# Token halves for the last two blocks of x, recounted scheduler costs and new ranks in a hybrid decoder layer

## The chip, the core and the metric

The kernel runs on one core of one Trainium2 chip. The metric is the device time of one execution in microseconds, as the median of three runs. The engines are TensorE (PE, with its weight loads as PEld), VectorE (DVE), ScalarE (ACT), GpSimd (POOL) and SyncE (SP), which issues all loads and stores here.

## The reference

One decoder layer over 1,024 tokens of width 1,024, in float32:

```python
mod = silu(c) @ w_ada + b_ada                    # shift, scale, gate, 1024 each
h = rms_norm(x, norm_w) * (1 + scale) + shift
u_pool, g_pool, q, k, v, g_attn, qi, ki, wi = split(h @ w_in)   # 2888 columns
pool_out = pool_mixer(u_pool, w_pool, pool_scale) * silu(g_pool)  # running means over 2, 4, 8, 16 tokens
q, k = rope(rms_norm(q)), rope(rms_norm(k)); qi, ki = rope(qi), rope(ki)
# per block of 128 queries: index scores, the 256 best keys of each query, softmax over those
score = sum_h relu(qi_h . ki) * wi_h;  sel = top_k(score, 256)
attn_out = softmax(q . k[sel]) @ v[sel] * silu(g_attn)
x = x + gate * (concat(pool_out, attn_out) @ w_out)
```

## The kernel before

The 1,024 channels of x lie in eight blocks of 128 partitions by 1,024 tokens (xt). The work comes in stages.

**Start.** `token_sums` (lines 505 to 564) loads x block by block, squares each block on ScalarE (sq), and adds the squares over all channels. A block in `SUMS` (0, 2, 4) goes to TensorE by itself as eight one-column products (128x1, one per 128 tokens, against a column of ones); the other blocks are first added on VectorE, and their sum goes to TensorE as eight more. The last block alone is loaded, squared and added in two token halves, tokens 512 to 1,023 first. `token_scales` turns the sums into 1/rms, by square root on ScalarE, reciprocal on VectorE and eight transposes on TensorE that spread it over the partitions (rsb). `lead_loads` and `modulations` meanwhile reduce the 16 blocks of w_ada (wa) for shift and scale on VectorE.

**Lead.** For each block j, `first_block` or `h_block` makes xn = x * rsb, then h as a high part (hhi) and a low part (hlo), so that a product can be had as three fast ones (hi*hi, hi*lo, lo*hi). `lead_line` then computes four tiles of the index queries over all eight blocks at once. GpSimd multiplies xn for blocks 1 to 7 and makes the low halves of the weights (wl); VectorE makes hlo. `SCALED` lists blocks whose xn is made on VectorE instead (none). Key and value rows follow.

**Middle.** `gates`, `queries` and `pool_mixer` compute the other projections in a fixed order, mixed with the index scores (kiT). The choice of the 256 best keys is a bisection over the bits of the score, on VectorE (junk) for query blocks 2 to 4 and on ScalarE (ajunk) for 5 to 7. `pool_mixer` ends in a high and a low part per group (mph, mpl).

**Attention and output.** `unit` does one query block: scores (kT,qr), a masked copy with row maxima on VectorE (ex, mx), exponentials on ScalarE, transposes of ex, and products with the values (pw,vrow). `gated` multiplies by the gate and splits the result (mah, mal). `output_line` runs beside it as filler: `project_pooled` first, then `project_attended(0)` for tokens 0 to 511 when query blocks 0 to 3 are done, and `project_attended(1)` at the very end.

**What sets the order.** The whole order is made when the program is built. Every strand of work is a generator that yields operations; `Flow.run` (line 415) takes at each step the strand whose operation can start first by a model of times, shifted by a rank: `EARLY` by name (or by name and number) for VectorE, ScalarE, GpSimd and SP, `LAST` by kind for TensorE, `SAFE` as a slack that a TensorE operation wants behind its data. `Op._cost` (line 150) holds the costs; `Op.data` (line 182) says when operands and outputs are free; `Either` picks between two engines with `FAVOUR` and `BACK`. Nothing of this runs on the chip: there the engines work through their lists in order and wait on semaphores.

All helper-issued instructions carry one line in the profile, L216 (L223 in the changed program), so that groups are told apart by tile names.

Of the kernel before, what the change touches and what calls it, by code (L numbers as in the profile page):

```python
# [17 lines left out]
P = 128  # L18
S = 1024
NT = 8  # L20
# [19 lines left out]
         "pick": -0.6, "mix": -0.33, "rotated": 0.12, "query_loads": 0.01, "exps": -0.11, "score_sums": -1.13,  # L40
         "key_value_out": -1.67, "index_queries": -1.47, "norm": -2.65, "gate_loads": 0.5, "token_scales": -0.26,
         "gate_mods": -0.39, "unit": -0.41, "index_scores": -0.67, "lead_loads": 1.25, "out": -1.53,
         "lead_out": -0.72, "weight_loads": -0.67, "key_value_weights": -0.07, "main_line": 0.66,
# [8 lines left out]
         "key_value_out 7": -1.92, "exps 5": -0.08, "key_value_out 4": -3.2, "query_norms": 0.51, "exps 8": 0.04,  # L52
# [7 lines left out]
         "products": -1.29, "shift 4": -0.32, "norm 5": -1.88, "low 1": -0.9, "turns 6": -2.43, "gated 6": -1.5,  # L60
         "turns 8": -2.26}
# [5 lines left out]
SAFE = {"side": 1.0, "unit": 0, "query_norms": 0, "h_block": 0.59, "rotated": 0.73, "query_loads": 0,  # L67
        "norm": 0.0, "weight_loads": 1.18, "key_value_out": 0.39, "turned": 0.26, "finish": 0.07, "index_keys": 0,
        "main_line": 0, "output_line": 0, "gate_mods": 1.07, "selection": 0, "low": 0, "maxima": 0,
        "attention": 0.05, "lead_out": 0, "score_relus": 0.1, "lead_loads": 0.28, "score_sums": 0.18, "mix": 0.96,  # L70
        "main": 0, "modulations": 0.09, "out": 0.39, "turns": 0, "exps": 0}
# [9 lines left out]
PHOP = -0.09  # L81
STT = 0.075
# [16 lines left out]
MIX = 4  # L99
# [20 lines left out]
class Op:  # L120


    def __init__(self, eng, name, fn, args, kw):
        self.eng, self.name, self.fn, self.args, self.kw = eng, name, fn, args, kw
        aps = [a for a in args if isinstance(a, bass.AP)]
        named = [a for k, a in kw.items() if isinstance(a, bass.AP)]
        self.outs, self.ins = [], []
        for a in aps[:1] + [kw[k] for k in ("accum_out",) if kw.get(k) is not None]:
            self.outs.append(store(a))
            if a.free_size() == 1:  # L130
                self.outs.append((store(a), a.offset))
# [18 lines left out]
    def _cost(self, aps, kw):  # L150
        size = [a.free_size() for a in aps]
        n = max(size)
        eng = self.eng
        if eng == "SP":
            return 0.42
        if eng == "PE":
            rate = 2 if self.name == "transpose" else 4 if aps[1].dtype == F32 else 1
            if self.name != "transpose" and min(aps[0].shape[0], aps[1].shape[0]) == 64:
                self.mode = "rows" if aps[1].shape[0] == 64 else "columns"
                return size[0] * 0.000417 * rate / 2 + 0.007  # L160
            return max(0.109, size[0] * 0.000417 * rate + 0.0135)
        wide = [a for a, k in zip(aps, size) if k == n]
        psum = any(a.space == PSUM for a in wide)
        half = all(mybir.dt.size(a.dtype) == 2 for a in wide)
        if eng == "ACT":
            t = 0.000833 * n + (0.05 if psum else 0.094)
            t += 0.093 * sum(isinstance(kw.get(k), bass.AP) for k in ("scale", "bias", "accum_out"))
            return t
        if eng == "POOL":
            if self.name == "tensor_tensor":  # L170
                return 0.0021 * n + 0.147
            return 0.000833 * n + 0.16
        if self.name in ("tensor_scalar", "tensor_copy"):
            if "accum_out" in kw:
                return 0.00104 * n + 0.13
            if half:
                return 0.00026 * n + 0.069
            if not psum:
                return 0.00052 * n + 0.069
        return 0.00104 * n + 0.069 + (STT if psum and self.name == "scalar_tensor_tensor" else 0.0)  # L180

    def data(self, flow):
# [4 lines left out]
        for a in self.outs:  # L187
# [209 lines left out]
def hybrid_layer(ctx, tc, xT, cT, nwT, badaT, wada, wq, wet, wkv, qnw, knw, wpool,  # L397
# [107 lines left out]
    def token_sums():  # L505
# [32 lines left out]
        halves = [slice(512, 1024), slice(0, 512)]  # L538
# [3 lines left out]
        added = [j for j in range(NT) if j not in SUMS]  # L542
        acc, started = None, set()
        for j in range(NT):
            sq = yield big(s="sq")
            for c in (halves if j == NT - 1 else [slice(0, 1024)]):
                yield A.activation(sq[:, c], xt[j][:, c], AF.Square)
                if j in added and acc is not None:
                    yield V.tensor_tensor(acc[:, c], acc[:, c], sq[:, c], op=OP.add)
                if j in SUMS or j == added[-1]:  # L550
                    t = sq if j in SUMS else acc
                    for h, half in enumerate(halves):
                        if half.start >= c.start and half.stop <= c.stop:
                            for b in range(4):
                                o = half.start + b * P
                                yield mm(tab["sums"][h][:, b:b + 1], t[:, o:o + P], ones,
                                         h not in started, j == NT - 1 and b == 3)
                                started.add(h)
            if j in SUMS or acc is not None:
                flow.drop(sq)  # L560
# [160 lines left out]
    def lead_line():  # L721
# [3 lines left out]
        for j in range(NT):  # L725
# [23 lines left out]
            flow.drop(whi, wlo)  # L749

# [29 lines left out]
    def weight_splits():  # L780
        for n in range(4 + 16 + 24):
# [678 lines left out]
    def main_line():  # L1460
        yield from lead_line()
# [27 lines left out]
    flow.spawn(weight_splits(), "weights")  # L1489
    flow.spawn(main_line(), "main")  # L1490
# [109 lines left out]
```

## Time and profile before

| | |
|---|---|
| median of 3 runs | 525.88 us (525.6 to 526.51) |
| the profiled execution | 525.81 us, its span 524.1 us |
| TensorE busy | 500.9 us, 96% of the span |
| VectorE, ScalarE, GpSimd busy | 421.7, 381.7, 134.9 us |
| mean granted TensorE clock | 0.993 |

A matmul's busy time overlaps that of the next one, so a busy TensorE is not TensorE at its peak; its waits are read from the view that lists what an engine waited for and from the order of time, where starts of neighbours can be compared.

### The profile page before, as it was taken

The page shows a single profiled execution, that of the slowest core. Times are in us where ns is not written, and L with a number is a line of the kernel's source. Part 1 is how long each engine was busy: PE and PEld are TensorE (multiplying, and loading weights), DVE is VectorE, ACT ScalarE, POOL GpSimd, SP SyncE. Part 2 cuts the span into 40 slices and gives each one's busy share as a digit, 9 for nine tenths or more (in the row PEclk, how much of TensorE's full clock was granted, in tenths as well). Part 3 has the DMA queues.
Part 4 walks back from the last instruction along what each step waited for, and adds up shares of the span by engine and source line. Part 5 has one row for each costly group of instructions (what it writes and reads, how often), then busy time and mean ns, then how long its engine had stood idle before and what let it go on. Part 6 is the DMA issues. An engine that isn't in the chain of part 4 may idle for free.

```text
span 524.1 us, 7765 instructions
## 1 busy us (share of the span) xinstructions
PE 500.9 (96%) x2568; PEld 380.8 (73%) x2568; DVE 421.7 (80%) x902; ACT 381.7 (73%) x868; POOL 134.9 (26%) x154
## 2 busy tenths in 40 slices
PE   6789999999999999989999997999998999999997
PEld 5778899767778868868878775886655756646585
DVE  1799895799789799999999998779896788975142
ACT  6488641687777989979953986899999826877520
POOL 1499430001001223345032431422210124200000
PEclk9999999999999999999999997999999999999999
DMA  8996513010214130211110114673521414301054
GB/s 307 403 408 214 203 45 115 22 61 21 83 28 153 41 87 34 81 40 42 41 41 20 40 43 149 200 250 125 181 82 41 141 60 155 107 21 41 1 161 161
DMA packets 28025, 58.31 MB, mean 111 GB/s; under 512 B 3792, under 2 KB 7888, under 8 KB 27984
## 3 DMA queue, kind: packets, MB, share of 16 engines
q1 hardware_dynamic: 27984, 57.81, 32.6%
q8 instruction: 20, 0.33, 0.3%
q14 instruction: 21, 0.17, 0.1%
HBM read 47.32 MB, written 10.49 MB: 110 GB/s over the span
## 4 chain that ended last, share of the span: by engine, by line
PE 61%; DVE 26%; ACT 7%; issue 4%; POOL 1%; DMA 1%; SPq 0%; DVEq 0%; ACTq 0%
PE m L216 61%; DVE junk L216 10%; ACT ex L216 3%; DVE selw L216 2%; DVE nx L216 2%; DVE sw L216 2%; DVE xq L216 1%; DVE ex L216 1%; DVE aq L216 1%; ACT ajunk L216 1%; DVE gp L216 1%; DVE wl L216 1%; DVE qr L216 1%; DVE mpl L216 1%; DVE u L216 1%
## 5 line engine op out<-in xcount | busy, mean ns | idle before, releaser
L216 PE MATMUL m<-hhi,wh 128*128 128x512 f32 (+1 forms) x320 | 120.3, 398 | 4.0 <-ACT hhi L216 4.0
L216 PE MATMUL m<-hhi,wl 128*128 128x512 f32 (+1 forms) x320 | 115.2, 382 | 0.0
L216 PE MATMUL m<-hlo,wh 128*128 128x512 f32 (+1 forms) x320 | 114.0, 380 | 0.0
L216 ACT ACTIVATE ajunk<-key,xq 128x768 bf16<-128x768 uint16 (+2 forms) x93 | 96.4, 1036 | 2.4 <-DVE xq L216 1.5
L216 PEld LDWEIGHTS m<-hhi,wh 128*128 128x128 f32 x320 | 59.0, 190 | 20.6 <-ACT hhi L216 4.9
L216 DVE TENSOR_SCALAR_CACHE_REDUCE junk<-key,xq 128x384 bf16<-128x384 uint16 (+2 forms) x93 | 69.1, 743 | 2.0
L216 PEld LDWEIGHTS m<-hhi,wl 128*128 128x128 f32 x320 | 59.3, 190 | 12.1 <-issue 1.4
L216 PEld LDWEIGHTS m<-hlo,wh 128*128 128x128 f32 x320 | 58.5, 188 | 12.4 <-DVE hlo L216 0.8
L216 POOL TENSOR_TENSOR wl<-ld,wh 128x512 fp32r<-128x512 f32 x38 | 54.0, 1423 | 43.7 <-ACT wh L216 35.5
L216 ACT ACTIVATE ex<-ex,mx,c 128x384 f32<-128x384 f32 (+7 forms) x64 | 54.9, 859 | 6.5 <-DVE mx L216 6.4
L216 ACT ACTIVATE kt<-m 128x512 f32<-128x512 f32 (+1 forms) x80 | 37.5, 526 | 10.6 <-DVE score L216 6.9
L216 DVE SCALAR_TENSOR_TENSOR score<-kt,c,score 128x1024 f32<-128x1024 f32 (+5 forms) x42 | 39.9, 950 | 6.5 <-ACT kt L216 4.4
L216 DVE SCALAR_TENSOR_TENSOR xo<-m,c,xo 128x512 f32<-128x512 f32 x28 | 21.0, 748 | 24.6 <-PE m L216 19.7
L216 PE MATMUL m<-kT,qr 64*128 64x512 f32 (+3 forms) x192 | 37.9, 512 | 1.6 <-DVE mx L216 1.5
L216 PE MATMUL m<-c,ex 128*128 128x128 f32 x288 | 34.4, 274 | 0.6 <-ACT ex L216 0.3
L216 PEld LDWEIGHTS m<-c,ex 128*128 128x128 f32 x288 | 31.5, 141 | 4.1 <-DVE mx L216 1.4
L216 ACT CAST wh<-ld 128x512 fp32r<-128x512 f32 x36 | 22.0, 615 | 16.3 <-PE m L216 10.8
L216 POOL TENSOR_SCALAR wh<-ld 128x512 fp32r<-128x512 f32 x23 | 15.7, 683 | 69.1 <-PE m L216 58.1
L216 PE MATMUL m<-pw,vrow 128*64 128x512 f32 x144 | 32.7, 598 | 0.0
L216 PEld LDWEIGHTS m<-kT,qr 64*128 64x128 f32 x192 | 18.6, 192 | 18.8 <-issue 11.0
L216 DVE CUSTOM_DVE_ANT_0 ex<-m,key 128x512 f32<-128x512 f32 (+1 forms) x48 | 30.9, 662 | 0.5 <-PE m L216 0.3
L216 PE MATMUL m<-mah,wh 128*128 128x512 f32 x64 | 25.8, 404 | 2.5 <-ACT mah L216 1.3
(190 smaller groups left out, 1036.5 us busy)
## 6 DMA issues: line engine op xcount, KB each, us to landing
wa<-wada SPq DMA_DIRECT2D x24, 512.0 KB, 7.5
ld<-wet SPq DMA_DIRECT2D x16, 512.0 KB, 3.3
ld<-wout SPq DMA_DIRECT2D x24, 256.0 KB, 2.8
xo<-xT SPq DMA_DIRECT2D x16, 256.0 KB, 3.4
y_d<-xo SPq DMA_DIRECT2D x16, 256.0 KB, 2.6
xo<-y_d SPq DMA_DIRECT2D x16, 256.0 KB, 3.3
outT<-xo SPq DMA_DIRECT2D x16, 256.0 KB, 2.2
xt<-xT SPq DMA_DIRECT2D x7, 512.0 KB, 6.6
```

The costliest lines, as they stand in the source:

```text
L216: self.fn(*self.args, **self.kw)
```

## The change

Three things are done, and the numbers that steer the scheduler are replaced throughout.

First, blocks 6 and 7 of x are loaded, squared and added in token halves: both second halves (tokens 512 to 1,023) first, then both first halves. `SUMS` becomes (1, 4), so that 24 one-column products stand where 32 stood.

```diff
-        for j in range(NT):
-            t = yield big(s="xt")
-            for c in ([slice(512, 1024), slice(0, 512)] if j == NT - 1 else [slice(0, 1024)]):
-                yield SP.dma_start(t[:, c], xT[j][:, c])
-            xt.append(t)
+        halves = [slice(512, 1024), slice(0, 512)]
+        pieces = [(j, slice(0, 1024)) for j in range(6)] + [(j, c) for c in halves for j in (6, 7)]
+        for j, c in pieces:
+            if len(xt) == j:
+                xt.append((yield big(s="xt")))
+            yield SP.dma_start(xt[j][:, c], xT[j][:, c])
...
+        sq, acc = {}, None
+        for j, c in pieces:
+            if j not in sq:
+                sq[j] = yield big(s="sq")
+            yield A.activation(sq[j][:, c], xt[j][:, c], AF.Square)
+            if j in SUMS:
+                yield from sums(sq[j], c, False)
+            elif acc is None:
+                acc = sq[j]
+                continue
+            else:
+                yield V.tensor_tensor(acc[:, c], acc[:, c], sq[j][:, c], op=OP.add)
+                if j == NT - 1:
+                    yield from sums(acc, c, True)
```

Second, the scheduler's model: a one-column product of float32 counts as 0.427 us, and an operation that writes one column of a table waits for that column's last users, not for the whole table's.

```diff
-        self.outs, self.ins = [], []
+        self.outs, self.ins, self.over = [], [], []
...
+            self.over.append(self.outs[-1] if a.space != PSUM else store(a))
...
-            return max(0.109, size[0] * 0.000417 * rate + 0.0135)
+            return max(0.427 if rate == 4 else 0.109, size[0] * 0.000417 * rate + 0.0135)
...
-        for a in self.outs:
+        for a in self.over:
             if self.eng == "PE":
```

Third, `lead_line` is a strand of its own that spawns `main_line` at its end, and the first four weight splits are a strand `lead_splits`, so that both have ranks of their own. Of the tables, a few lines:

```diff
-SCALED = ()
+SCALED = (7,)
-SUMS = (0,2,4,)
+SUMS = (1, 4,)
...
-LAST = {"main": 0.12, "fill": 0.113, "scores": -0.039, "attend": -0.078, "evac": -0.027, "qi": 0.284,
-        "side": -0.239}
+LAST = {"main": 0.12, "fill": -0.037, "scores": 0.035, "attend": -0.085, "evac": -0.027, "qi": 0.294,
+        "side": -0.55}
...
-QK = 3
-IK = 3
+QK = 2
+IK = 1
...
-PV = 3
+PV = 5
```

The order that comes out differs on every engine. Three places follow, as the built program lists them.

VectorE right behind the token sums (c_93 is 1/rms, wa a block of w_ada, xn and hlo those of block 0). Before:

```order
L216 RECIPROCAL c_93<-c_93 128x4
L216 SCALAR_TENSOR_TENSOR wa_209,c_89<-wa_209,m 128x1024
L216 RECIPROCAL c_93<-c_93 128x4
L216 SCALAR_TENSOR_TENSOR wa_211,c_89<-wa_211,m 128x1024
L216 TENSOR_SCALAR c_89<-c_89,c_78 128x1
L216 SCALAR_TENSOR_TENSOR wa_214,c_89<-wa_214,m 128x1024
L216 SCALAR_TENSOR_TENSOR xn_243<-xt_108,c_90,m 128x512
L216 SCALAR_TENSOR_TENSOR wa_219,c_89<-wa_219,m 128x1024
L216 SCALAR_TENSOR_TENSOR hlo_245<-xn_243,c_89,hhi_244 128x512
L216 SCALAR_TENSOR_TENSOR wa_221,c_89<-wa_221,m 128x1024
```

Now:

```order
L223 RECIPROCAL c_93<-c_93 128x4
L223 SCALAR_TENSOR_TENSOR wa_205,c_89<-wa_205,m 128x1024
L223 TENSOR_SCALAR c_90<-c_89,c_78,c_77 128x1
L223 SCALAR_TENSOR_TENSOR wa_207,c_89<-wa_207,m 128x1024
L223 SCALAR_TENSOR_TENSOR xn_252<-xt_108,c_90,m 128x512
L223 RECIPROCAL c_93<-c_93 128x4
L223 SCALAR_TENSOR_TENSOR hlo_254<-xn_252,c_89,hhi_253 128x512
L223 SCALAR_TENSOR_TENSOR xn_252<-xt_108,c_90,m 128x512
L223 SCALAR_TENSOR_TENSOR wa_210,c_89<-wa_210,m 128x1024
L223 SCALAR_TENSOR_TENSOR hlo_254<-xn_252,c_89,hhi_253 128x512
```

Block 0 (both halves of xn and hlo) now stands behind two or three blocks of w_ada, not behind three to seven.

The low parts of the pooled mixer, at the start of attention (mph_3297 and mph_3332 are group 0, which the output projection reads first). Before, on VectorE:

```order
L216 CAST mph_3297<-gp_2904 128x1024
L216 TENSOR_SCALAR junk_3287,cq_692_3280<-key_85,xq_688_3266 128x640
L216 ISA ex_3299,mx_2669<-m,mask_82 128x128
L216 ISA mx_2669 128x1
L216 ISA ex_3299,mx_2669<-m,mask_82 128x128
L216 ISA mx_2669 128x1
L216 ISA ex_3296,mx_2671<-m,mask_82 128x256
L216 ISA mx_2671 128x1
L216 TENSOR_TENSOR mpl_3301<-gp_2366,mph_3300 128x1024
L216 ISA ex_3299,mx_2669<-m,mask_82 128x128
L216 ISA mx_2669 128x1
L216 TENSOR_TENSOR mpl_3298<-gp_2904,mph_3297 128x1024
```

Now, on GpSimd:

```order
L223 TENSOR_SCALAR wh_3294<-ld_3167 128x512
L223 TENSOR_SCALAR yq_706_3316<-xq_690_3269 128x3
L223 TENSOR_TENSOR wl_3295<-ld_3167,wh_3294 128x512
L223 TENSOR_TENSOR mpl_3336<-gp_2681,mph_3335 128x1024
L223 TENSOR_TENSOR mpl_3333<-gp_2887,mph_3332 128x1024
```

Group 0's low part has moved from VectorE to GpSimd, behind a weight chunk and behind group 3's low part.

TensorE behind the last query block (pw,vrow), where the final output projection begins. Before:

```order
L216 MATMUL m<-pw_4997,vrow_643 64x512 x2
L216 MATMUL m<-pw_5008,vrow_643 64x512 x2
L216 MATMUL m<-mah_4419,wh_4542 128x512
L216 MATMUL m<-mah_4419,wl_4543 128x512
L216 MATMUL m<-mal_4420,wh_4542 128x512
```

Now:

```order
L223 MATMUL m<-pw_4993,vrow_637 64x512 x2
L223 MATMUL m<-mah_3851,wh_4820 128x512
L223 MATMUL m<-mah_3851,wl_4821 128x512
L223 MATMUL m<-mal_3852,wh_4820 128x512
L223 MATMUL m<-mah_3851,wh_4820 128x512
L223 MATMUL m<-mah_3851,wl_4821 128x512
L223 MATMUL m<-mal_3852,wh_4820 128x512
L223 MATMUL m<-mah_4465,wh_4843 128x512
```

Six products of tokens 0 to 511 (mah_3851, ready since query block 3) now stand between the last attention products and the first product that needs the last query block (mah_4465). In the same way eight kT,qr products stand behind query block 3, where mah followed at once; and of the 96 products of `project_attended(0)` fewer stand beside query blocks 4 and 5, more beside 6 and 7.

## Rows read from the trace of the kernel before

**Rows 1.** The page's first line and its part 1: busy time of an engine, share of the span, instructions.

```profile
span 524.1 us, 7765 instructions
...
PE 500.9 (96%) x2568; PEld 380.8 (73%) x2568; DVE 421.7 (80%) x902; ACT 381.7 (73%) x868; POOL 134.9 (26%) x154
```

**Rows 2.** TensorE alone in a stretch of the lead: stretch, its length, busy time (instructions), granted clock as a share of full, share of the DMA engines, GB/s.

```profile
33.00:62.50 29.50, 29.50 (x170) 1.00 0.71 254
```

**Rows 3.** The start in order of time (all engines): start us, length us, engine, line, operation, written tile <- read tiles, shapes, how many were merged, and in brackets the idle time before it and what ended that. sq are squares of a block, c small constants (here also the scale of the tokens), m is PSUM.

```profile
7.15 13.79 PE L216 MATMUL m<-c,sq 128*128 128x1 f32 x64 [0.52 <-ACT sq L216]
...
9.31 1.06 ACT L216 ACTIVATE sq<-xt 128x1024 f32<-128x1024 f32 x1 [0.22 <-DMA xt<-xT]
...
10.59 1.06 ACT L216 ACTIVATE sq<-xt 128x1024 f32<-128x1024 f32 x1 [0.22 <-DMA xt<-xT]
...
12.96 3.96 DVE L216 TENSOR_TENSOR sq<-sq,sq 128x1024 f32<-128x1024 f32 x4 [1.33 <-ACT sq L216]
...
19.27 0.26 ACT L216 ACTIVATE c<-m,c 128x4 f32<-128x4 f32 x1 [4.01 <-PE m L216]
...
20.80 1.95 PE L216 MATMUL m<-c,c 128*128 128x128 f32 x8
...
23.86 0.74 DVE L216 SCALAR_TENSOR_TENSOR xn<-xt,c,m 128x512 f32<-128x512 f32 x1
...
25.41 2.08 PE L216 MATMUL m<-hhi,wh 128*128 128x512 f32 x4 [2.67 <-ACT hhi L216]
...
30.30 0.74 PE L216 MATMUL m<-hhi,wh 128*128 128x256 f32 x4 [1.30 <-ACT hhi L216]
```

**Rows 4.** ScalarE in the same view, the two half squares of the last block.

```profile
14.13 1.13 ACT L216 ACTIVATE sq<-xt 128x512 f32<-128x512 f32 x2
```

**Rows 5.** VectorE alone in two stretches, columns as in rows 2: the lead, and the stretch up to the start of attention.

```profile
21.30:58.70 37.40, 36.71 (x49) 1.00 0.80 296
186.00:319.00 133.00, 129.04 (x291) 1.00 0.16 50
```

**Rows 6.** Groups of instructions of VectorE in the lead: count, busy us, mean ns of one, idle time before them.

```profile
L216 DVE SCALAR_TENSOR_TENSOR wa<-wa,m 128x1024 f32<-128x1024 f32 x15 | 17.9, 1209 | 0.0
L216 DVE TENSOR_TENSOR hlo<-xn,hhi 128x1024 fp32r<-128x1024 f32 x7 | 11.8, 1691 | 0.5 <-ACT xn L216 0.5
```

**Rows 7.** GpSimd's groups in the lead, same columns.

```profile
L216 POOL TENSOR_TENSOR xn<-xt,rsb 128x1024 f32<-128x1024 f32 x7 | 20.2, 2893 | 0.0
L216 POOL TENSOR_TENSOR wl<-ld,wh 128x512 fp32r<-128x512 f32 x7 | 12.5, 1793 | 0.0
```

**Rows 8.** End of the lead, VectorE, then (next group) TensorE, in order of time.

```profile
57.45 1.21 DVE L216 TENSOR_TENSOR hlo<-xn,hhi 128x1024 fp32r<-128x1024 f32 x1
```

**Rows 9.** TensorE at the same place: the first product that reads the low half of the last block.

```profile
58.72 0.50 PE L216 MATMUL m<-hlo,wh 128*128 128x512 f32 x1
```

**Rows 10.** What TensorE waited for over the whole span: us in total, times, longest.

```profile
PE m L216 <- DVE u L216: 1.8, 2, 1.5
PE m L216 <- DVE mx L216: 1.5, 1, 1.5
PE m L216 <- DVE mpl L216: 1.5, 1, 1.5
PE m L216 <- ACT mah L216: 1.3, 1, 1.3
PE m L216 <- DVE mah L216: 1.2, 1, 1.2
PE m L216 <- ACT pw L216: 0.7, 1, 0.7
```

**Rows 11.** TensorE at the start of attention, in order of time. kT,qr are the first attention scores, mph and mpl the output projection's first inputs.

```profile
313.81 1.37 PE L216 MATMUL m<-kT,qr 64*128 64x128 f32 x16
...
317.83 0.40 PE L216 MATMUL m<-mph,wl 128*128 128x512 f32 x1
319.69 0.80 PE L216 MATMUL m<-mpl,wh 128*128 128x512 f32 x1 [1.47 <-DVE mpl L216]
```

**Rows 12.** GpSimd at the same place: a weight chunk's high half, and its low half.

```profile
311.25 0.62 POOL L216 TENSOR_SCALAR wh<-ld 128x512 fp32r<-128x512 f32 x1 [0.93 <-PE m L216]
...
313.77 1.27 POOL L216 TENSOR_TENSOR wl<-ld,wh 128x512 fp32r<-128x512 f32 x1
```

**Rows 13.** VectorE at the same place.

```profile
318.42 2.35 DVE L216 TENSOR_TENSOR mpl<-gp,mph 128x1024 fp32r<-128x1024 f32 x2
```

**Rows 14.** TensorE in three stretches there, columns as in rows 2.

```profile
315.00:320.00 5.00, 2.06 (x11) 0.88 0.83 250
320.00:325.00 5.00, 5.00 (x14) 0.50 0.33 117
325.00:330.00 5.00, 5.00 (x29) 0.94 0.34 105
```

**Rows 15.** TensorE after the attention of query block 3: pw,vrow are its last products, mah the next work.

```profile
398.98 3.65 PE L216 MATMUL m<-pw,vrow 128*64 128x512 f32 x16
403.85 0.50 PE L216 MATMUL m<-mah,wh 128*128 128x512 f32 x1 [1.21 <-DVE mah L216]
```

**Rows 16.** TensorE after the attention of the last query block, same columns.

```profile
492.44 4.46 PE L216 MATMUL m<-pw,vrow 128*64 128x512 f32 x20
498.16 0.50 PE L216 MATMUL m<-mah,wh 128*128 128x512 f32 x1 [1.25 <-ACT mah L216]
```

More of the change, by code (lines that the diff above doesn't have):

```diff
@@ L39 @@
          "mods": -0.2, "select": -0.1, "scores": -0.6, "attend": -1.1, "late": 1.0, "kv": -0.3, "qi": -0.8,
[L40 to L43, printed above, removed]
@@ L44 @@
-         "output_line": -0.14, "turns": -1.46, "finish": -1.64, "index_keys": -1.47, "h_block": 0.28,
-         "attention_keys": -0.36, "turned": -1.72, "h_blocks": -0.3, "gated": -2.15, "modulations": -0.22,
-         "low": -0.4, "gear": -0.3, "attention": 0.31, "maxima": -0.99, "score_relus": -0.66, "gated 7": -1.82,
[5 rows of a table removed]
-         "key_value_out 7": -1.92, "exps 5": -0.08, "key_value_out 4": -3.2, "query_norms": 0.51, "exps 8": 0.04,
[7 rows of a table removed]
-         "products": -1.29, "shift 4": -0.32, "norm 5": -1.88, "low 1": -0.9, "turns 6": -2.43, "gated 6": -1.5,
@@ L61 @@
-         "turns 8": -2.26}
+         "pick": -0.6, "mix": -0.33, "rotated": 1.0, "query_loads": -0.28, "exps": -0.11, "score_sums": -1.13,
+         "key_value_out": -1.67, "index_queries": -1.47, "norm": -1.6, "gate_loads": -1.2, "token_scales": -3.22,
+         "gate_mods": -0.39, "unit": -0.41, "index_scores": -0.91, "lead_loads": 0.74, "out": -1.53,
+         "lead_out": -0.72, "weight_loads": 0.17, "key_value_weights": 0.67, "main_line": 0.66, "output_line": 0.91,
+         "turns": -1.46, "finish": -1.64, "index_keys": -1.47, "h_block": 0.28, "attention_keys": -0.36,
@@ new lines @@
+         "turned": -1.01, "h_blocks": -2.07, "gated": -2.15, "modulations": -0.38, "low": 0.65, "gear": -0.3,
+         "attention": -0.86, "maxima": -0.99, "score_relus": -0.66, "gated 7": -1.82, "gated 3": -1.0,
[5 rows of a table added]
+         "key_value_out 7": -1.92, "exps 5": -0.25, "key_value_out 4": -3.2, "query_norms": 0.16, "exps 8": 0.04,
[7 rows of a table added]
+         "gear 4": 0.68, "products": -1.29, "shift 4": -0.32, "norm 5": -1.86, "low 1": -2.52, "turns 6": -2.43,
+         "gated 6": -1.5, "turns 8": -1.76, "h_block 3": 0.04, "shift": -0.01, "gear 8": -2.5, "lead_line": 1.29,
@@ L63 @@
+         "gear 7": -1.58, "index_queries 3": -3.45, "index_queries 1": -2.08, "lead_splits": -0.23, "shift 5": -0.05,
+         "first_block": -2.64, "shift 2": 0.74, "lead_out 1": -1.22, "shift 8": 1.3, "out 7": -0.3, "unit 3": -1.17,
+         "turns 3": -2.02, "key_value_out 1": -2.25, "exps 4": -0.27, "mix 2": -0.25}
 SELECT = -0.366
-LAST = {"main": 0.12, "fill": 0.113, "scores": -0.039, "attend": -0.078, "evac": -0.027, "qi": 0.284,
-        "side": -0.239}
+LAST = {"main": 0.12, "fill": -0.037, "scores": 0.035, "attend": -0.085, "evac": -0.027, "qi": 0.294,
+        "side": -0.55}
@@ L67 @@
 SAFE = {"side": 1.0, "unit": 0, "query_norms": 0, "h_block": 0.59, "rotated": 0.73, "query_loads": 0,
[L68 to L71, printed above, removed]
@@ L73 @@
-SCALED = ()
-SUMS = (0,2,4,)
-WKM = 5
+        "norm": 0, "weight_loads": 1.18, "key_value_out": 0.39, "turned": 0.26, "finish": 0.07, "index_keys": 0,
+        "main_line": 0, "output_line": 0, "gate_mods": 1.06, "selection": 0, "low": 0.27, "maxima": 0,
+        "attention": 0.44, "lead_out": 0, "score_relus": 0, "lead_loads": 0.28, "score_sums": 0.18, "mix": 0.96,
+        "main": 0, "modulations": 0.09, "out": 0.39, "turns": 0.34, "exps": 0, "lead_line": 0.6, "shift": 0,
+        "token_scales": 0.08, "index_scores": 0.19, "products": 0, "index_queries": 0.34}
@@ L80 @@
+SCALED = (7,)
+SUMS = (1, 4,)
+WKM = 6
 HOP = 0.103
-PHOP = -0.09
-STT = 0.075
+PHOP = -0.148
+STT = 0.078
 HOPS = {"PE": 0.19, "DVE": 0.13, ("ACT", "DVE"): 0.14, ("ACT", "ACT"): 0.035}
@@ L87 @@
 AGE = 0.37
-PW_POOL = 0.303
+PW_POOL = 0.088
 XO_POOL = 0.108
-BACK = 0.5
-SPAN = 0.115
-QK = 3
-IK = 3
+BACK = 0.768
+SPAN = 0.104
+QK = 2
+IK = 1
 FK = 0
 PK = 0
-MIX = 4
+GM = 4
+MIX = 5
 KEEP = 7
 FLY = 2
-PV = 3
-WA_AHEAD = 5
-AHEAD = 2
+PV = 5
+WA_AHEAD = 3
+AHEAD = 5
 XN_AHEAD = 2
-FAVOUR = {"DVE": 0.235, "ACT": -0.057, "POOL": 0.244}
+FAVOUR = {"DVE": 0.245, "ACT": -0.062, "POOL": 0.244}
 TABLES = {AF.Silu: 1, AF.Sqrt: 2, AF.Exp: 3}
@@ L536, in token_sums @@
         tab["scp"] = psum[:, 0:1024]
-        halves = [slice(512, 1024), slice(0, 512)]
         tab["sums"] = []
@@ L541, in token_sums, with sums @@
             tab["sums"].append((yield bank(4)))
[L542 to L560, printed above, removed]
-            else:
-                acc = sq
-            if j == added[-1]:
-                flow.drop(acc)
+        started = set()
+        def sums(t, c, last):
+            for h, half in enumerate(halves):
+                if half.start >= c.start and half.stop <= c.stop:
+                    for b in range(4):
+                        o = half.start + b * P
+                        yield mm(tab["sums"][h][:, b:b + 1], t[:, o:o + P], ones, h not in started, last and b == 3)
+                        started.add(h)
+        sq, acc = {}, None
[8 more added lines that the diff above has]
+                continue
+            else:
+                yield V.tensor_tensor(acc[:, c], acc[:, c], sq[j][:, c], op=OP.add)
+                if j == NT - 1:
+                    yield from sums(acc, c, True)
+            if c.start == 0:
+                flow.drop(sq[j])
+        flow.drop(acc)
     def token_scales():
@@ L749, in lead_line @@
             flow.drop(whi, wlo)
+        flow.spawn(main_line(), "main")
     def lead_out(e, acc):
@@ L778, in weight_loads, with lead_splits, weight_splits @@
             loaded.append((t, 512, 1))
-    def weight_splits():
-        for n in range(4 + 16 + 24):
+    def lead_splits():
+        yield from weight_splits(range(4))
+        flow.spawn(weight_splits(range(4, 4 + 16 + 24)), "weights")
+    def weight_splits(which):
+        for n in which:
             yield lambda: len(loaded) > n
@@ L1460, in main_line @@
     def main_line():
-        yield from lead_line()
         kv["v"] = yield big(s="vrow")
@@ L1488, in hybrid_layer @@
     flow.spawn(weight_loads(), "weights")
-    flow.spawn(weight_splits(), "weights")
-    flow.spawn(main_line(), "main")
+    flow.spawn(lead_splits(), "weights")
+    flow.spawn(lead_line(), "main")
     flow.spawn(gate_mods(), "late")
```

2 lines of the change are left out of this document (1 added, 1 removed), and 24 rows, old and new, of the table EARLY.

## The prediction

> **What bounds the kernel now.** The profiled execution took 525.81 us, 0.07 below the median of 525.88, so a sum made against the one holds for the other. About 0.2%, 1.05 us, is what a measurement of this kernel can tell from no change.
>
> I began with the busy times. TensorE is busy in 96% of the span [rows 1]: no edit here takes products of the main work away, so time can come only from where TensorE stands idle or runs at less than its full clock. Second I read the start in order of time. Blocks of x land 1.28 us apart (squares begin at 9.31 and 10.59), but TensorE's one-column products run without a gap from 7.15 to 20.94; the 64 records are 32 products (the float32 ones leave two records each), so one takes 13.79 / 32 = 0.431 us. The sums are bound by the number of products, not by the loads: the last half squares are done at 15.26 [rows 4], the first square root comes at 19.27, the transposes at 20.80, block 0's xn at 23.86 and TensorE's first main product at 25.41, with a hole before 30.30 [rows 3].
>
> Third, what feeds the lead. TensorE has no gap from 33.0 to 62.5 [rows 2], but VectorE is busy 36.71 of 37.40 us there [rows 5]. Its last low half begins at 57.45 and ends at 58.66 [rows 8]; the product that reads it begins at 58.72 [rows 9]. Most of VectorE's time is in 15 blocks of w_ada at 1.209 and 7 hlo at 1.691 [rows 6], GpSimd's in 7 xn at 2.893 and 7 wl at 1.793 [rows 7]. So the lead ends when VectorE is done, and an earlier start counts in full only if VectorE's list also starts earlier or gets shorter.
>
> Fourth, the list of what TensorE waited for: u 1.8, mx 1.5, mpl 1.5, and mah twice, 1.3 and 1.2 [rows 10]. Before attention VectorE is busy 129.04 of 133 us [rows 5], so that the middle too hangs on it as much as on TensorE. Fifth, the order of time around the waits, and the windows there: the mpl wait ends at 319.69 [rows 11], and the granted clock is 0.88, 0.50 and 0.94 in the three windows of 5 us from 315 on, after TensorE had been busy for only 2.06 of the first five [rows 14].
>
> **The change part by part.** *Sums.* Eight products fewer is 8 x 0.431 = 3.45 us. Block 1 is squared about 0.85 later than block 0, so TensorE starts that much later. From there: block 1 from 8.0 to 11.45, block 4 (square from 10.59 to 11.65) from 11.7 to 15.1. Then the last four products of a half wait for the adds; those of the last five blocks now begin at 12.96 and last 3.96 [rows 3], half adds half of that. With the second halves of blocks 6 and 7 first, I estimate that half's sum for 15.8, its four products till 17.5, the other four till 19.2. The first square root can come at 17.6 for 19.27: **1.7 us earlier**, and 2.6 (3.45 - 0.85) if the adds never make TensorE wait.
>
> That two more transfers now are halves costs little: the two half squares of the last block ran from 14.13 to 15.26 back to back [rows 4]. The Trainium skill ("DMA: Bandwidth & Descriptors", section "Anatomy of one DMA — SWDGE (gpsimd) path") gives each DMA a fixed cost of about 2.0 us beside its bytes. By it, if the queue showed that cost for the one DMA added, the sum below would be some 523.3; no such 2 us lie between the halves in rows 4.
>
> *Lead.* Block 0 stands ahead of more of w_ada on VectorE, so the first main product should gain about another 1.1, starting near 22.6. But VectorE ends the lead. It starts 1.7 earlier; it loses one hlo (to GpSimd, 1.69) and the blocks that go behind the lead (one, 1.21), and gains one xn of the nearest kind (two inputs, 1.21): 1.7 less. As xn of block 0's first half now waits for the second square root and transposes, I put in one new wait of 1.3, the size of the hole before 30.30 [rows 3]. Together -1.7 - 1.7 + 1.3 = **-2.1 us**, bounds 0 (all of it swallowed) and -3.4 (no new wait). GpSimd is given one hlo and loses one xn at 2.893 [rows 7], so I count its queue at nothing; if hlo6 came late there, the price is the upper bound.
>
> *Middle.* New ranks, and VectorE gets two products of the index queries from GpSimd, while it gives up low parts of the pooled mixer. I count **-0.5**: a part of the 1.8 for u [rows 10]. Bounds: -1.8, and +1.5, a wait as long as the longest of them.
>
> *Start of attention.* The wait for mpl goes from VectorE to GpSimd. Now VectorE makes two mpl in 2.35 from 318.42 [rows 13]. GpSimd had wh at 311.25 and wl from 313.77 to 315.04 [rows 12]; behind it come two low parts of 128x1024, between twice a VectorE one (2.4) and twice its own wl (3.6): ready between 319.8 and 322 if gp and mph are there. More kT products stand before mph, which fills some of that. I take **0**, bounds -1.5 and +2.1, and the clock falls as now.
>
> *After query blocks 3 and 7.* TensorE waited 1.21 before 403.85 [rows 15] and 1.25 before 498.16 [rows 16]. Eight products of scores, and six old mah products of 0.5 each (3 us), now lie in these holes; their data are long there. The work is moved, not added: **-2.5**, bounds -2.5 and 0 (if the hole opens where they were taken from).
>
> *Fillers held back.* project_attended(0) now runs later, so query blocks 4 to 6 have less beside them while exponentials and transposes are awaited. I count one more wait of pw's size [rows 10]: **+0.7**, bounds 0 and +4.
>
> The scheduler's recounted costs do nothing on the chip but through the order. The sum: -2.1 - 0.5 + 0 - 2.5 + 0.7 = -4.4, so 525.8 - 4.4 = **521.4 us**.
>
> **The rivals.** *(a) The forecast*, lead and both covers.
>
> *(b) Only the lead's gain reaches the end.* The covers are paid for by holes beside the later query blocks: 525.8 - 2.1 = 523.7. For it: filler is finite. Against it: the moved products are few, and TensorE has few short waits in attention [rows 10].
>
> *(c) Nothing arrives.* VectorE's list before attention is nearly full [rows 5]: TensorE's earlier start only makes it wait longer for u, and the covers are paid for as in (b): 525.8. Against: the lead's list on VectorE itself gets shorter.
>
> *(d) Slower.* One mechanism: the held-back filler. If TensorE beside query blocks 4 to 6 has nothing else while exponentials run, it waits there, as it did for mx (1.5), and after a stretch of idle the clock falls as it did from 318 to 326, which cost 5 x (0.12 + 0.50 + 0.06) = 3.4 us [rows 14]. Three waits of 1.5 and one such fall are 7.9 in place of 0.7: 521.4 + 7.2 = 528.6. It decides for slower from about 5.5 us of new holes on. For it: the order does thin the filler out there. Against: the wait list has so little in attention that some slack must be there.
>
> *(e) More gained.* The clock stays up at the start of attention, as kT products fill it and the mpl wait of 1.5 is gone: 521.4 - 3.4 - 1.5 = 516.5. Against: TensorE was busy 2.06 of 5 us there [rows 14], more than these products fill.
>
> *(f) The halves land late.* If a transfer more holds the loads up by as long as a block takes, 1.28 [rows 3], the last half is squared 1.3 later, and the gain of the lead falls from 2.1 to 0.8: 522.7. Rows 4 speak against it. The rule on DMAs named above would ask for this kind of loss, and more.
>
> *(g) GpSimd's new subtractions and VectorE get in each other's way.* The same subtraction hlo took 1.691 on average in the lead, beside a full GpSimd [rows 6], and mpl 1.18 at the start of attention [rows 13]: 0.5 for each instruction. Two low parts on GpSimd beside four or five VectorE operations would cost 2.4: 523.8. The Trainium skill ("SBUF — State Buffer", section "SBUF: two separate sides") has it that the port VectorE and GpSimd share goes to one of them for a whole instruction while the other blocks; the two lengths of that subtraction agree with a loss, though with a partial one.
>
> **How the numbers follow.** Chances: (a) 0.44, (b) 0.16, (c) 0.10, (d) 0.12, (e) 0.08, (f) 0.05, (g) 0.05. The predicted time is (a)'s, 521.4. The forecast's own range goes from 525.8 - 3.4 - 1.8 - 2.5 = 518.1, all bounds on the good side and no new wait, to (b)'s 523.7. The range given reaches from 518.0 to 526.0: (b), (c), (f) and (g) lie in it, and (d) and (e), 0.20, outside. Faster by over 0.2% are (a), (b), (e), (f) and (g), 0.78; within 0.2% is (c), 0.10; slower is (d), 0.12.
>
> **What would show it.** Sums: 24 one-column products that end near 19.2, a first square root near 17.6. Lead: a first main product near 22.6, the key and value rows beginning about two us earlier, VectorE's last hlo or xn still just ahead of TensorE. Start of attention: a wait for mpl now on GpSimd, a window at about half clock. After query blocks 3 and 7: no wait for mah. The forecast is wrong if the start of the key and value rows does not move, if waits for ex, pw or mx beside query blocks 4 to 6 sum to over 3 us, or if a second stretch at half clock appears.

## The result, and the profile after

Median of six runs 522.58 us (521.29 to 524.34) beside 525.85 for the kernel before: ratio 0.9935, 95% interval 0.9914 to 0.9956. The profiled execution took 522.8, its span is 521.1 for 524.1 [rows 1]:

```profile
span 521.1 us, 7755 instructions
...
PE 500.1 (96%) x2552; PEld 378.4 (73%) x2552; DVE 419.7 (81%) x898; ACT 382.6 (73%) x871; POOL 137.0 (26%) x159
```

The start in order of time, columns as in [rows 3]. Here the records of one-column products come in three pieces:

```profile
7.50 1.06 ACT L223 ACTIVATE sq<-xt 128x1024 f32<-128x1024 f32 x1 [0.62 <-DMA xt<-xT]
...
8.70 3.54 PE L223 MATMUL m<-c,sq 128*128 128x1 f32 x16 [2.19 <-ACT sq L223]
...
12.46 3.58 PE L223 MATMUL m<-c,sq 128*128 128x1 f32 x16 [0.22 <-ACT sq L223]
...
16.62 3.57 PE L223 MATMUL m<-c,sq 128*128 128x1 f32 x16 [0.59 <-DVE sq L223]
...
18.53 0.26 ACT L223 ACTIVATE c<-m,c 128x4 f32<-128x4 f32 x1 [2.48 <-PE m L223]
...
23.21 2.06 PE L223 MATMUL m<-hhi,wh 128*128 128x512 f32 x4
```

16 records (eight products) run from block 1 at 8.70, 16 from block 4, and the last 16 wait 0.59 for VectorE's sums. The first square root is at 18.53 for 19.27 and the first main product at 23.21 for 25.41 [rows 3]. But block 1 was squared only at 7.50, and block 2 at 8.79; in the trace of before block 2 was squared at 8.03.

The end of the lead on TensorE: the hlo that GpSimd now makes, and the first key and value rows.

```profile
55.02 1.66 PE L223 MATMUL m<-hlo,wh 128*128 128x512 f32 x8 [0.38 <-POOL hlo L223]
...
61.11 0.32 PE L223 MATMUL m<-wkh,hhi 128*128 128x328 f32 x1
```

The key and value rows began at 62.57 before, so the lead ends **1.46 us earlier**. What TensorE waited for over the span (us in total, times, longest):

```profile
PE m L223 <- DVE mx L223: 4.0, 4, 2.1
...
PE m L223 <- DVE qsl L223: 1.3, 1, 1.3
...
PE m L223 <- POOL hlo L223: 0.4, 1, 0.4
```

Of [rows 10] u, mpl and both mah are gone; mx has gone from 1.5 to 4.0, qsl from 0.3 to 1.3. TensorE behind the last query block has no wait ahead of mah, where [rows 16] had 1.25:

```profile
486.83 7.09 PE L223 MATMUL m<-pw,vrow 128*64 128x512 f32 x32
493.85 0.50 PE L223 MATMUL m<-mah,wh 128*128 128x512 f32 x1
```

The last main projection (hlo) ends 0.82 earlier than before, the last product 2.94. So in this execution the gain was 1.46 at the end of the lead, fell by 0.64 in the middle, and grew by 2.1 in attention and output.

The start of attention holds the surprise. VectorE, GpSimd and TensorE there, each in order of time, and TensorE's windows [rows 14]:

```profile
312.60 0.16 DVE L223 TENSOR_TENSOR aq<-cq,kcq 128x3 f32<-128x3 f32 x1
312.68 1.29 DVE L223 CAST mph<-gp 128x1024 fp32r<-128x1024 f32 x2
313.88 2.32 DVE L223 SCALAR_TENSOR_TENSOR xq<-aq,yq 128x3 f32<-128x3 f32 x1
316.13 0.28 DVE L223 CUSTOM_DVE_ANT_0 ex<-m,mask 128x128 f32<-128x128 f32 x1
```

```profile
313.45 5.04 POOL L223 TENSOR_TENSOR mpl<-gp,mph 128x1024 fp32r<-128x1024 f32 x2 [0.98 <-DVE mph L223]
```

```profile
312.99 1.36 PE L223 MATMUL m<-kT,qr 64*128 64x128 f32 x14
316.47 1.67 PE L223 MATMUL m<-kT,qr 64*128 64x128 f32 x12 [2.12 <-DVE mx L223]
```

```profile
315.00:320.00 5.00, 3.35 (x18) 0.81 0.71 220
320.00:325.00 5.00, 5.00 (x12) 0.51 0.30 95
325.00:330.00 5.00, 5.00 (x23) 1.00 0.25 87
```

An operation on 128x3 elements, xq, a step of the bisection, lasts 2.32 us and ends at 316.20. The GpSimd record merges two mpl; the first of them ended at 316.18. All row maxima (ex) stand behind xq, and TensorE's scores wait 2.12 us for them; then the clock is at half, as before. The wait for mpl went, and this one took its place.

### The profile page after: what moved, and what is told of

The parts are those of the page before. It is cut to its first block, busy times and chain, and to the rows that moved or that the text cites. A ratio compares the mean times of both kernels' runs of the same rounds, so it can differ in the third digit from the quotient of the medians.

```text
span 521.1 us, 7755 instructions
## 1 busy us (share of the span) xinstructions
PE 500.1 (96%) x2552; PEld 378.4 (73%) x2552; DVE 419.7 (81%) x898; ACT 382.6 (73%) x871; POOL 137.0 (26%) x159
## 4 chain that ended last, share of the span: by engine, by line
PE 67%; DVE 14%; ACT 7%; issue 4%; DMA 2%; POOL 1%; SPq 0%; DVEq 0%; ACTq 0%; POOLq 0%
PE m L223 67%; DVE junk L223 4%; DVE ex L223 2%; ACT ajunk L223 1%; DMA ld<-wq 1%; DVE score L223 1%; DMA wa<-wada 1%; DVE wa L223 1%; DVE xq L223 1%; ACT kt L223 1%; ACT ex L223 1%; DVE nx L223 1%; ACT st L223 1%; POOL wl L223 1%; ACT hhi L223 1%
## 5 line engine op out<-in xcount | busy, mean ns | idle before, releaser
L223 ACT ACTIVATE ex<-ex,mx,c 128x256 f32<-128x256 f32 (+7 forms) x64 | 55.0, 864 | 9.0 <-DVE mx L223 8.9
L223 POOL TENSOR_TENSOR wl<-ld,wh 128x512 fp32r<-128x512 f32 x36 | 51.4, 1431 | 35.6 <-ACT wh L223 30.4
L223 DVE SCALAR_TENSOR_TENSOR xo<-m,c,xo 128x512 f32<-128x512 f32 x26 | 19.5, 750 | 24.4 <-PE m L223 17.5
L223 ACT COPY pw<-m 128x512 f32<-128x512 f32 x47 | 24.9, 612 | 6.8 <-PE m L223 6.8
```

The source lines that it names most:

```text
L223: self.fn(*self.args, **self.kw)
```

## The experiments

To move one thing and nothing else, the scheduler's sequence of steps in the changed kernel was written down, with its choice of engine and PSUM bank at each, and is replayed in place of its decisions. All kernels below but new_sums_before are that sequence with single steps moved. Times are medians; ratios are to runs of the kernel before on the same chip.

**again** and **xq_first**: the sequence as it is, and with one instruction moved.

```diff
 TENSOR_TENSOR aq_704<-cq_694,kcq_251 128x3
+SCALAR_TENSOR_TENSOR xq_705<-aq_704,yq_706 128x3
 CAST mph_3335<-gp_2681 128x1024
 CAST mph_3337<-gp_2382 128x1024
-SCALAR_TENSOR_TENSOR xq_705<-aq_704,yq_706 128x3
 ISA ex_3334,mx_2648<-m,mask_82 128x128
```

> The changed kernel once more, its order written out and held. In the first trace of the change the second block of x was squared at 7.50 us, in that of before at 6.91; everything in the head came 0.76 later than the edit alone would have it. If that was chance of one execution, this trace has block 1 at about 6.9 and the first main product near 22.5; if it belongs to the change, 7.5 and 23.2 again. Time 521.3 to 524.3, median 522.6.

> One VectorE instruction moved: the bisection's three-element xq stands before the two casts mph, not behind them, so that it runs before GpSimd's first low part mpl begins. In the change it lasted 2.32 us (313.88 to 316.20), until GpSimd's mpl ended at 316.18, and TensorE's scores waited 2.1 us for the row maxima behind it. Theory of the port (an operation of VectorE with two operands in SBUF stands still while GpSimd's runs): xq takes 0.17, the wait of 2.1 goes, and the time falls by 2.1, or by up to 5.5 if the half clock from 316 on (3.4) goes too. Rival (the maxima were late for another reason): xq moves, the maxima still begin at about 316, no change of time.

again: 521.91 (519.69 to 522.84), ratio 0.9909 [0.9886, 0.9931]; block 1 was squared at 7.63, so the late loads came again. xq_first: **516.99** (516.39 to 518.59), ratio 0.9832 [0.9812, 0.9852]. That is 4.9 us by the medians and 4.1 by the ratios for one three-element instruction; in the traces, products behind 327 us come 4.0 earlier than in the change, measured against those ahead of 314. The same places in xq_first:

```profile
312.72 0.16 DVE L223 SCALAR_TENSOR_TENSOR xq<-aq,yq 128x3 f32<-128x3 f32 x1
312.80 1.29 DVE L223 CAST mph<-gp 128x1024 fp32r<-128x1024 f32 x2
314.00 0.28 DVE L223 CUSTOM_DVE_ANT_0 ex<-m,mask 128x128 f32<-128x128 f32 x1
...
315.19 0.61 DVE L223 TENSOR_SCALAR_CACHE_REDUCE junk<-key,xq 128x384 bf16<-128x384 uint16 x1
```

```profile
313.56 5.05 POOL L223 TENSOR_TENSOR mpl<-gp,mph 128x1024 fp32r<-128x1024 f32 x2 [1.25 <-DVE mph L223]
```

```profile
314.35 1.67 PE L223 MATMUL m<-kT,qr 64*128 64x128 f32 x12 [0.16 <-DVE mx L223]
...
318.67 0.50 PE L223 MATMUL m<-mpl,wh 128*128 128x512 f32 x1 [0.55 <-POOL mpl L223]
```

```profile
315.00:320.00 5.00, 4.27 (x24) 1.00 0.69 222
320.00:325.00 5.00, 5.00 (x24) 1.00 0.42 148
325.00:330.00 5.00, 5.00 (x24) 1.00 0.69 216
```

GpSimd's two mpl last as long as in the change, but xq, done before they begin, takes 0.16. The maxima begin at 314.00 for 316.13, TensorE's wait is 0.16 for 2.12, and the granted clock stays full. The maxima (one operand from PSUM) and the one-operand pass at 315.19 run beside GpSimd at their usual length. The Trainium skill ("SBUF — State Buffer", section "SBUF: two separate sides") says that GpSimd and a VectorE operation with two SBUF inputs lock each other out for a whole instruction; xq has two, and its end 0.02 behind GpSimd's agrees, in full and not in part as the prediction's rival (g) took it.

**mpl_dve**: xq where the change has it, both mpl chosen for VectorE.

```diff
 (VectorE, among the row maxima)
+TENSOR_TENSOR mpl_3336<-gp_2681,mph_3335 128x1024
+TENSOR_TENSOR mpl_3333<-gp_2887,mph_3332 128x1024
 (GpSimd)
-TENSOR_TENSOR mpl_3336<-gp_2681,mph_3335 128x1024
-TENSOR_TENSOR mpl_3333<-gp_2887,mph_3332 128x1024
```

> The change itself (xq where it was), but the two low parts mpl at the start of attention on VectorE, where before had them, not on GpSimd. By the theory of the port xq takes 0.17 at 313.9; but VectorE now has two operations of 1.2 more among the maxima. The wait of 2.1 for the maxima shrinks to about 1.2, and a wait for mpl comes in its place: 521 to 522.5, as the change. If GpSimd had nothing to do with the wait, it is 2.4 longer than in the change: 524.

522.62 (521.49 to 524.05), ratio 0.9917 [0.9903, 0.9931]. VectorE:

```profile
313.84 0.15 DVE L223 SCALAR_TENSOR_TENSOR xq<-aq,yq 128x3 f32<-128x3 f32 x1
...
314.54 1.22 DVE L223 TENSOR_TENSOR mpl<-gp,mph 128x1024 fp32r<-128x1024 f32 x1
...
317.32 1.22 DVE L223 TENSOR_TENSOR mpl<-gp,mph 128x1024 fp32r<-128x1024 f32 x1
```

At the same place in the same order xq takes 0.15 once GpSimd is idle: GpSimd's occupation was the cause. The time stays, since the two mpl now cost VectorE 1.22 each among the maxima, and the window from 320 to 325 shows a clock of 0.54. So mpl on GpSimd was worth its move only once xq no longer stood beside it: 516.99 in xq_first.

**wl_dve** (on xq_first): one low part of a weight chunk goes from GpSimd to VectorE, behind qsl.

```diff
 (VectorE)
 TENSOR_TENSOR aq_343<-cq_332,kcq_251 128x3
+TENSOR_TENSOR wl_1968<-ld_1760,wh_1967 128x512
 (GpSimd)
-TENSOR_TENSOR wl_1968<-ld_1760,wh_1967 128x512
```

The place in the change, VectorE and GpSimd, and TensorE's window behind it:

```profile
189.44 0.42 DVE L223 CAST qsh<-st 128x512 fp32r<-128x512 f32 x1
189.90 1.64 DVE L223 TENSOR_TENSOR qsl<-st,qsh 128x512 fp32r<-128x512 f32 x1
```

```profile
189.49 1.51 POOL L223 TENSOR_TENSOR wl<-ld,wh 128x512 fp32r<-128x512 f32 x1
```

```profile
192.00:198.00 6.00, 6.00 (x22) 0.74 0.45 132
```

> xq_first with one low part of a weight chunk (wl, 128x512) made on VectorE instead of GpSimd, behind qsl. In the change GpSimd's wl ran from 189.49 to 190.99, VectorE's qsl from 189.90 to 191.54 (0.96 longer than its like), and TensorE waited 1.28 for it, after which the granted clock fell in two of three profiles. Theory of the port: qsl takes 0.69 and the wait falls to 0.33, so 0.96 to 2.5 below xq_first (516.0 to 514.5). Rival (qsl was slow for its own operands, or VectorE's added 0.7 comes back as a later wait): within 0.3 of 517.0.

517.49 (516.85 to 518.94), ratio 0.9833 [0.9816, 0.9849]. qsl takes 0.69 again:

```profile
190.42 0.69 DVE L223 TENSOR_TENSOR qsl<-st,qsh 128x512 fp32r<-128x512 f32 x1
```

and TensorE's wait for it is 0.33 for 1.28. That GpSimd's wl held qsl is shown, but the median did not move, because the hold came back elsewhere. Set beside again, whose clock did not fall at 192 us either, wl_dve gains 0.96 at qsl and loses 0.83 of it by 227 us:

```profile
224.24 1.29 POOL L223 TENSOR_TENSOR wl<-ld,wh 128x512 fp32r<-128x512 f32 x1
```

```profile
224.42 2.18 DVE L223 SCALAR_TENSOR_TENSOR u<-nx,u 128x1024 f32<-128x1024 f32 x1
```

```profile
226.66 1.12 PE L223 MATMUL m<-u,c 128*128 128x512 f32 x2 [0.57 <-DVE u L223]
```

GpSimd's next wl now begins 0.18 ahead of u, a step of the pooled mixer that TensorE waits for. In again u began 0.20 ahead of that wl and took 1.22, and the wl took 2.17. This is the later wait that the rival foresaw, by another way.

The clock adds its own scatter. In this profile it fell behind the wait for maxima (0.72 in the window from 390 to 396), which cost 1.6; the profile of xq_first had a fall at 192 (0.72 in that window), and that fall is most of the 1.7 by which products at 232 us come earlier here, against the key and value rows. Where it falls differs between executions of one program: in again, with the same 1.28 us of wait as in the change, the window behind it shows

```profile
192.00:198.00 6.00, 6.00 (x28) 1.00 0.46 167
```

for 0.74 in the change.

**selw_late** (on xq_first): a VectorE operation of 1.17 us moved behind four row maxima.

```diff
-SCALAR_TENSOR_TENSOR selw<-selw,needq,sg 128x768
 RECIPROCAL sume<-sume 128x8
 ...
 ISA ex_4183,mx_4117<-m,key_85,mx_4117 128x128
+SCALAR_TENSOR_TENSOR selw<-selw,needq,sg 128x768
```

> xq_first with one VectorE instruction moved: selw (128x768, 1.17 us at 389.4) of the next selection stands behind four row maxima of query block 5, not ahead of them. In the change TensorE's transposes waited 1.28 us for a maximum (at 395.2; 391.0 in xq_first) that stood behind it. If that wait is the held-back filler's price and is VectorE's order alone: wait down to 0.3, time 1 us below xq_first, 516.0. Rival (the transposes need the exponentials, on ScalarE): TensorE waits for ex instead, and the time stays at 517.0.

517.38 (517.26 to 517.57), ratio 0.9827 [0.9813, 0.9841]: no gain that can be told. TensorE's transposes:

```profile
388.09 0.33 PE L223 MATMUL m<-c,ex 128*128 128x128 f32 x1 [0.39 <-ACT ex L223]
389.40 0.65 PE L223 MATMUL m<-c,ex 128*128 128x128 f32 x4 [0.98 <-DVE mx L223]
```

The wait was 0.38 and 1.28, it is 0.39 and 0.98. selw was 0.3 of it. Most of the rest is VectorE's own wait for the exponentials, right ahead of the maximum in question, so the rival holds for that part:

```profile
388.87 0.20 DVE L223 RECIPROCAL sume<-sume 128x8 f32<-128x8 f32 x1 [0.65 <-ACT ex L223]
```

**tail_undone** (on xq_first): the six old mah products stand ahead of the last pw,vrow again.

```diff
+MATMUL m<-mah_3851,wh_4820 128x512   (and the five behind it)
 MATMUL m<-pw_4897,vrow_637 64x512 x2
 ...
 MATMUL m<-pw_4993,vrow_637 64x512 x2
-MATMUL m<-mah_3851,wh_4820 128x512   (and the five behind it)
 MATMUL m<-mah_4465,wh_4843 128x512
```

> The kernel xq_first (516.99) with one thing undone: the six old mah products stand ahead of the last query block's last products again, not behind them. If they cover the wait for mah: TensorE waits about 1.25 us behind the last pw,vrow (as before at 498.16), and the time is 1.2 to 1.3 above xq_first, 518.2. Rival (the work is only moved, the wait was short of nothing): the six products lie elsewhere, the wait stays hidden, 517.0.

519.69 (518.62 to 520.27), ratio 0.9868 [0.9853, 0.9884], so about 1.9 above xq_first by the ratios. In the traces the last product comes 1.32 later, measured against products at 480 us, as was expected. The wait is back to the hundredth:

```profile
491.98 0.50 PE L223 MATMUL m<-mah,wh 128*128 128x512 f32 x1 [1.25 <-ACT mah L223]
```

**new_sums_before** and **old_sums**: the token sums alone, put into the order of before, and taken out of that of the change. **best_old_sums** takes them out of best (below), where the clock rarely falls. The edit is the first diff of the change, or its reverse, with `SUMS`.

> The kernel before with its whole order held, but the new token sums. If the sums carry the gain: 0.7 to 1.7 below before (524.2 to 525.2), key and value rows at 60.9 to 61.9 for 62.6. Rival (VectorE's list ends the lead whatever the sums do): no change, 525.6 to 526.1.

> The changed kernel with its whole order held, but the token sums of before: 32 one-column products, halves of the last block alone. If the sums carry the gain of the lead: first square root 0.7 to 1.7 later, key and value rows as much later, and the time 0.7 to 1.7 above the change (523.3 to 524.3). Rival (the gain of the lead comes from the new order on VectorE): the first main product is later, but the key and value rows and the end stay within 0.3 of the change.

> The kernel best (517.04, few falls of the clock) with the token sums of before and everything else held. On the change itself the same edit gave 523.67 beside 521.91, but with 519 to 526 over its executions, since the clock fell in a varying number of places. If the sums are worth what the first square root moves (0.7 to 1.3): 517.7 to 518.3. Rival (the lead ends when GpSimd's hlo of block 6 or VectorE is done, whatever the sums do): within 0.3 of best.

new_sums_before: 525.43, ratio 0.9983 [0.9970, 0.9995]; first square root 17.99, key and value rows 61.40, 1.17 earlier than before. old_sums: 523.67, ratio 0.9949 [0.9926, 0.9972], too scattered (519.14 to 525.99) to part from again; its trace has the square root 0.99 and the rows 0.74 later than the change. best_old_sums: 517.74 (517.62 to 517.92), ratio 0.9852 [0.9838, 0.9865] beside best's 0.9827; square root 19.25 for 18.05, rows 61.62 for 60.91. By the traces the sums are worth 0.7 to 1.2 us at the rows, or 0.4 to 1.4 at equal loads (block 2 was squared 0.25 later in new_sums_before than in before, and 0.28 later in best_old_sums than in best). VectorE's list did not swallow them: in the order of before 1.17 of 1.28 arrived at the rows, in the new order 0.71 of 1.20. By the times, only new_sums_before shows a gain; the intervals of best_old_sums and best overlap.

**xq_again** and **best** (xq_first with wl_dve's and selw_late's moves), on one chip:

> xq_first once more, beside the next kernel on the same chip: 516.4 to 518.6, ratio to before 0.983 again, no stretch at half clock between 312 and 324 us; in some executions one near 192 or 390.

> xq_first with both further moves: wl on VectorE, selw behind four maxima. Each alone took its wait away and left the time within 0.5 of xq_first, but each alone left the other place where the clock fell in some executions (wl_dve at 390 to 396, xq_first at 192 to 198). If those falls were what the waits cost, no execution has one: 516.0 to 516.7, spread under 0.5. Rival (the two moves cost VectorE as much as they save): as xq_first, 517.

xq_again 518.80 (516.30 to 519.16), ratio 0.9843 [0.9820, 0.9865]; best 517.04 (516.23 to 517.97), ratio 0.9827 [0.9812, 0.9842]. best kept a mean clock of 0.998 or 0.999 in all its runs, xq_again 0.995 to 0.998; its median is 1.8 lower, its interval overlaps. The expected spread under 0.5 did not come: the four runs of best lie 1.7 apart at almost the same clock, so falls of the clock are not the whole scatter, and its trace has the wait for u again, 0.58. best is about 5 us below the change and 9 below the kernel before.

**best_hlo**: best with block 6's hlo chosen for VectorE, where before had it.

```diff
 (VectorE)
+TENSOR_TENSOR hlo_505<-xn_430,hhi_504 128x1024
 (GpSimd)
-TENSOR_TENSOR hlo_505<-xn_430,hhi_504 128x1024
```

> best with the low half hlo of block 6 on VectorE, where before had it, not on GpSimd. In best GpSimd's hlo ran from 52.38 to 54.77 and TensorE waited 0.7 for it; VectorE had gaps of 1.9 and 0.2 shortly ahead. If the lead now ends on that hlo: it ends about 1.1 us earlier, the wait goes and the key and value rows begin 0.4 to 0.8 earlier, time 516.3 to 516.6. If VectorE ends the lead, as the prediction had it: its later wkl and last hlo come 1.2 later and the rows begin up to 1 us later, 517 to 518.

517.55 (516.65 to 517.66), ratio 0.9844 [0.9831, 0.9857]: not to be told from best. TensorE at the end of the lead, in best and then in best_hlo:

```profile
54.82 1.66 PE L223 MATMUL m<-hlo,wh 128*128 128x512 f32 x8 [0.68 <-POOL hlo L223]
...
60.91 0.32 PE L223 MATMUL m<-wkh,hhi 128*128 128x328 f32 x1
```

```profile
55.44 1.69 PE L223 MATMUL m<-hlo,wh 128*128 128x512 f32 x8 [0.17 <-DVE hlo L223]
...
61.58 0.32 PE L223 MATMUL m<-wkh,hhi 128*128 128x328 f32 x1
```

The wait fell from 0.68 to 0.17, but this execution's loads were late (block 1 at 8.14, square root 19.13 for 18.05). From square root to rows it is 42.45 us for 42.86 in best. But again, xq_first and tail_undone, whose lead has the order of best, took 42.33, 42.40 and 42.34 with waits of 0.17 to 0.22 for GpSimd's hlo: the long wait belongs to the execution of best that was profiled, and no gain of the move is shown.

## Why the prediction was right, and where it was not

The time (521.4 foreseen, 522.58 measured) and the sign came out; the terms did so unevenly. The agreement is in part luck: the start of attention came out by two things that cancel, and what the later stages gave depends on where the clock fell in the profiled execution. There the lead fell short by 0.6 and the middle by 1.1, and attention and output gave 0.3 more than foreseen. In again, the same program, the lead gave -1.61, the middle -0.89, attention and output -0.81. One sign that the prediction had named for being wrong did appear: a second stretch at half clock (0.74 in the window from 192 to 198).

- **Sums, -1.7 foreseen, -0.74 here.** At equal loads the step holds: blocks 2 onwards were squared 0.76 later than before, and 18.53 - 0.76 = 17.77 for the 17.6 foreseen. In new_sums_before, with loads 0.25 later, it was 17.99. What failed is that the loads were taken to land as before. Over twelve profiles in the order of the change block 1 was squared between 7.08 and 8.14, in two in the order of before at 6.91 and 7.05, with old sums or new. Its load was issued at 1.70 or 1.71 in all fourteen. Whether the order has a part in it stays open; two halves more are not the cause (old_sums had 7.74). Neither rival (f), the late halves, nor the 2 us that the prediction weighed for one more DMA shows: the half squares begin at 13.62, 14.14, 14.69 and 15.41. Two readings were loose: the squares of blocks 0 and 1 are 0.94 apart in the trace of before, not 0.85, and the 3.96 us of adds [rows 3] are blocks 5, 6 and the halves of 7, not five blocks.
- **Rest of the lead, -0.4 foreseen (-1.7 + 1.3).** From the first square root to the key and value rows it was 43.30 in before and 43.41 in new_sums_before, 42.58 in the change: -0.72. VectorE did not go on ending the lead: it is busy 33.13 of the 37.40 us of [rows 5], where it was 36.71. GpSimd, counted at nothing, makes TensorE wait 0.38 for hlo, and 0.15 to 0.68 in other executions. Both together -1.46 for -2.1.
- **Middle, -0.5 foreseen, +0.64 in the change, -0.89 in again.** The waits for u did go. The two executions differ by a fall of the clock behind qsl, which cost 1.56 (products at 232 us stand 1.68 earlier in again, where it did not fall, and were only 0.12 earlier at 188). It came in five of the seven profiles with that wait of 1.28, not in again and old_sums. What the term left out is that work on one engine can hold work on another: GpSimd's wl held VectorE's qsl for 0.95 more. The trace of before had such a hold to show, on an xq that takes 0.16 at 193 us:

```profile
187.99 1.13 DVE L216 SCALAR_TENSOR_TENSOR xq<-aq,yq 128x3 f32<-128x3 f32 x1
```

```profile
187.79 1.30 POOL L216 TENSOR_TENSOR wl<-ld,wh 128x512 fp32r<-128x512 f32 x1
```

- **Start of attention, 0 foreseen.** The sum was right by two things that cancel. mpl was ready at 318.49, earlier than the 319.8 to 322 foreseen, and its wait went; xq's 2.3 us put one of 2.12 in its place and kept the fall of the clock. Rival (g) priced this port at 2.4 for the subtractions themselves; the price fell on what waited beside them. Rival (e), 516.5 for a start without wait and fall, is close to what xq_first then gave, 516.99.
- **Covers, -2.5 foreseen.** The last one is shown by tail_undone: 1.25 of wait, 1.3 us in the traces and some 1.9 by the ratios. The one behind query block 3 was not tried alone, so its worth is not shown; there the trace has 0.45 for maxima in place of 1.21.
- **Fillers held back, +0.7 foreseen.** Beside query blocks 3 and 4 new waits of 0.39, 1.28 and 0.45 came, below the 3 us that would have made rival (d).

## What to carry over

A saving on one engine is to be followed on the engine that shares a port with it: look in the order of time for a tiny operation that lasts as long as another engine's large one, and move it out of the way, which here was worth more than the whole change (4.0 to 4.9 us against 3.3). Then look where the collision goes next: in wl_dve it went from qsl to u. Single instructions of a computed order are best tried by holding the rest of the order fixed. A wait of TensorE is to be priced with the half clock that may follow it.

## What the runs showed of the hardware

A 128x3 operation of VectorE with two operands in SBUF took 0.15 to 0.17 us alone and 2.32 beside a GpSimd subtraction of 128x1024; several of its kind in the middle took 0.9 to 1.1 more beside GpSimd's wl. A cast with one operand was held as well: in selw_late qsh took 1.31 for 0.42 beside that wl, so the count of operands is not the whole rule. GpSimd is held too: its wl took 2.17 for 1.29 in again, where VectorE's u began 0.20 earlier.

The same program ran from 521.29 to 524.34 us: the two runs at 521.3 had a mean granted clock of 0.992, the one at 524.34 0.987. The places are those where TensorE had waited a microsecond or two: behind qsl, at the start of attention, behind the maxima at 393. At the first the clock of one window was 0.74 in one execution and 1.00 in another, after the same wait of 1.28, and a fall there cost 1.6 us. Where the waits were shortened (best, best_old_sums) it hardly fell. The five runs of best_old_sums then lie within 0.3 us, the four of best within 1.7; what scatters them is open.
